# DeltaNet's triangular inverse in one decoder step: diagonal blocks of 32 instead of 16 solved on VectorE, and turned there

## Chip, core and metric

One NeuronCore of one Trainium2 chip runs the whole step as one program. The metric is the device time of one launch in microseconds (us). The engines carry the names of the profile: PE is TensorE (its weight loads are PEld), DVE is VectorE, ACT is ScalarE, POOL is GpSimd, and SP is the engine that issues every DMA of this kernel.

## What is computed

One layer of a decoder with three kinds of heads: 6 mLSTM heads (A), 6 gated DeltaNet heads (B) and 4 HGRN2 heads (C). The input is a prompt of 1024 tokens with 16 learned tokens in front of it, and 8 samples of 8 tokens. One projection of 2048 to 8984 columns gives all q, k, v and gate columns, and an output projection of 2048 x 2048 follows. Only the DeltaNet part is touched. Cut to what matters:

```python
def _gdn_segment(q, k, v, g, beta, S0, chunk):
    ...
    G = jnp.cumsum(gc, axis=-1)
    decay = jnp.exp(jnp.where(incl, G[..., :, None] - G[..., None, :], NEG_BIG))
    A = jnp.where(strict, bc[..., None] * decay * jnp.einsum('nbhtd,nbhsd->nbhts', kc, kc), 0.0)
    M = A + jnp.eye(c, dtype=A.dtype)
    rhs = jnp.concatenate([bc[..., None] * vc, (bc * jnp.exp(G))[..., None] * kc], axis=-1)
    sol = lax.linalg.triangular_solve(M, rhs, left_side=True, lower=True)
    U, Wk = sol[..., :HEAD_DIM], sol[..., HEAD_DIM:]
    ...
```

The kernel works in chunks of 128 tokens and builds the inverse of the unit triangular 128 x 128 matrix M of each chunk; the product of that inverse with the right-hand side follows.

## The kernel before

The tokens are worked through in two halves. The first half holds 592 columns: 512 prompt tokens in four chunks of 128, the 64 sample tokens and the 16 learned tokens (these 80 are a small fifth group). The second half holds the other 512 prompt tokens, four chunks. In each half the projection runs over the columns of the weights, head by head, in the order of `ORDER` (L39).

**The weight stream.** A piece is a 128 x 512 tile of weights. SP loads it into `wraw`, ACT rounds it to `whi`, DVE takes the rest into `wlo`, and PE multiplies the activations by both into `acc`. A piece is 24 matmuls in the first half (two accumulators) and 12 in the second. `wraw`, `whi` and `wlo` have four buffers each; `feed_ahead` (L273) splits three pieces ahead of PE and loads seven ahead.

**The heads' own work** runs beside this stream. Every head is a Python generator that issues a step and yields; `Weave` (L145) resumes it when a clock of estimated costs (`Clock`, L85, and `Engine.cost`, L112) says that its last step should be done. So PE's queue holds stream matmuls with a few matmuls of a head between them. PE works through its queue in order. The framework's scheduler then decides, before the run, in which order the instructions stand on the other engines.

**The inverse of a DeltaNet head** is in `gdn_scan` (from L1097). `Ball` holds the strictly triangular part B of M, for all chunks side by side (C of them: 5 in the first half, 4 in the second).

1. Each 16 x 16 diagonal block of B is written to DRAM (`db`, L1157, eight small DMAs), and its rows are read back so that each row stands in all partitions of its block (`Bb`, L1163, three DMAs).
2. `substitute()` solves all the diagonal blocks at once on DVE. `Yc` starts as an identity of 16 columns in each block, and 15 steps follow; each is a product `Yt` of a column of `Yc` with a row from `Bb`, and a subtraction from `Yc`. Each instruction needs the one before it. This is called the chain below.
3. One DVE instruction spreads `Yc` into the block-diagonal matrix Y (tag `s8`) with `submask`. After `substitute` the clock gets 8 us before the next step is issued.
4. `transpose_Y` turns the four chunks of Y on PE (`px`), ACT copies them to X (tag `s9`).
5. Doubling from 16 to 32: four full matmuls `pz` (B with X), DVE masks them with `zmask` into Z, four full matmuls `pyy`, DVE subtracts them from Y, and `transpose_Y` turns Y once more.
6. Doublings from 32 to 64 and from 64 to 128, with block matmuls `pz` and `pyy`; in the first of them `pyy` is computed for both X and Y.

Then a loop over the chunks carries the state (`pr`, `pw`, `pu`, `po`). In the first half, `first_chain` (the 80 tokens of the small group) is issued in pieces between the steps of the inverse. Before the inverse, `side()` issues `pqk` and the transposes `pvb` of v.

Of the kernel before, what the change touches and what calls it, by code (L numbers as in the profile page):

```python
# [6 lines left out]
F32 = mybir.dt.float32  # L7
F32R = mybir.dt.float32r
U8 = mybir.dt.uint8
BF16 = mybir.dt.bfloat16  # L10
AF = mybir.ActivationFunctionType
ALU = mybir.AluOpType
AX = mybir.AxisListType

P = 128
# [174 lines left out]
def hybrid_step(ctx, tc, i, o):  # L190
    nc = tc.nc
    ck = Clock()
    V, S, G, T = (Engine(ck, n, e) for n, e in (("V", nc.vector), ("S", nc.scalar), ("G", nc.gpsimd), ("T", nc.tensor)))
    DMA = nc.sync.dma_start
    weave = Weave(ck)

    cp = ctx.enter_context(tc.tile_pool(name="cp", bufs=1))
# [24 lines left out]
    ident = cp.tile([P, P], F32, name="ident")  # L222
# [284 lines left out]
    segment_mask(sm0, 1.0, 0.0, True)  # L507

    hmask = {}
    zmask = cp.tile([P, P], BF16, name="zmask")  # L510
    m = sq("io", "zm")
    G.memset(m, 0.0)
    v = m.rearrange("p (b x) -> p b x", x=2 * SUB)[:, :, 0:SUB]
    G.memset(v, 1.0)
    G.affine_select(v, v, pattern=[[-2 * SUB, P // (2 * SUB)], [0, SUB]], compare_op=ALU.is_ge, fill=0.0, base=-SUB, channel_multiplier=1)
    G.affine_select(v, v, pattern=[[2 * SUB, P // (2 * SUB)], [0, SUB]], compare_op=ALU.is_ge, fill=0.0, base=2 * SUB - 1, channel_multiplier=-1)
    G.tensor_copy(zmask, m)
# [28 lines left out]
    for r in range(0, P, 32):  # L546
        v = quadmask[r:r + 32]
# [4 lines left out]
    for r in range(0, P, NSAMP):  # L552
        v = rowmask[r:r + NSAMP]
# [39 lines left out]
    rows_dram = [dp.tile([5, HA, h], F32, name=f"rows{h}") for h in (WA, WB)]  # L593
# [173 lines left out]
        return cols_of[half.index][0:g.n, g.idx, kind, h:h + 1].to_broadcast([g.n, g.nt, width])  # L767

    def bc_row(tag, name, half, arr, h):
        t = row(tag, name)[:, 0:half.width]  # L770
        DMA(t, rows_dram[half.index][arr, h:h + 1, :].partition_broadcast(P))
        return t


# [322 lines left out]
    def gdn_scan(half, h, ck_, cq, cv, zs, Gb, eG, bb, st):  # L1097
        W = half.width
        gs, main = half.ggroups, half.gmain
        cols = cols_of[half.index]  # L1100
# [48 lines left out]
        for g, B in zip(gs, Bs):  # L1149
            n = g.n  # L1150
# [1 line left out]
            for c in range(g.nt):  # L1152
                T.matmul(g.psum(pk, n)[:, c], g.col(knT, c), g.col(knT, c), start=True, stop=True)
            V.tensor_tensor(B[0:n, :, 0:n], B[0:n, :, 0:n], g.psum(pk, n), op=ALU.mult)
        db = dp.tile([P // SUB, SUB, C, SUB], F32, name=f"db{half.index}{h}")
        for j in range(P // SUB):
            DMA(db[j], Ball[SUB * j:SUB * (j + 1), 0:C, SUB * j:SUB * (j + 1)])  # L1157
        dbf = db.rearrange("j s c t -> j (s c t)")
        Bb = []
        for lo, hi, tag in ((0, 6, "s7"), (6, 12, "s9"), (12, 15, "s6")):  # L1160
            w = C * SUB
            t = sp.tile([P, 512], F32, tag=tag, name="Bb", bufs=1)[:, 0:(hi - lo) * w]
            DMA(t, dbf[:, lo * w:hi * w].unsqueeze(1).to_broadcast([P // SUB, SUB, (hi - lo) * w]))  # L1163
            for x in range(hi - lo):
                Bb.append(t[:, x * w:(x + 1) * w].rearrange("p (c t) -> p c t", t=SUB))
        ready = ck.t["T"] + 7.0
        if half.first:
            kq = pair_tile()
# [4 lines left out]
        Ys, Xs = [], []  # L1173

        def transpose_Y(g, Y, X):
            n = g.n
            px = bank("px")
            for c in range(g.nt):
                T.transpose(g.psum(px, n)[:, c], Y[0:n, c, 0:n], ident[0:n, 0:n])
            S.copy(X[0:n, :, 0:n], g.psum(px, n))  # L1180

        def substitute():
            Yc = sp.tile([P, 5, SUB], F32, tag="Yc", name="Yc", bufs=1)[:, 0:C]
            tmp = sp.tile([P, 5, SUB], F32, tag="Yt", name="Yt", bufs=1)[:, 0:C]
            V.tensor_copy(Yc, subid.unsqueeze(1).to_broadcast([P, C, SUB]))
            for s_ in range(SUB - 1):
                r = slice(s_ + 1, SUB)
                V.tensor_tensor(tmp[:, :, r], Yc[:, :, s_:s_ + 1].to_broadcast([P, C, SUB - 1 - s_]), Bb[s_][:, :, r], op=ALU.mult)
                V.tensor_tensor(Yc[:, :, r], Yc[:, :, r], tmp[:, :, r], op=ALU.subtract)
                if s_ in (4, 9):  # L1190
                    ck.last = 0.0
                    yield
            for g in gs:
                nb = g.n // SUB
                Y = gt("8", g)
                V.tensor_tensor(Y[0:g.n, :, 0:g.n].rearrange("p c (j t) -> p c j t", t=SUB),
                                Yc[0:g.n, g.idx].unsqueeze(2).to_broadcast([g.n, g.nt, nb, SUB]),
                                submask[0:g.n, 0:g.n].rearrange("p (j t) -> p j t", t=SUB).unsqueeze(1).to_broadcast([g.n, g.nt, nb, SUB]),
                                op=ALU.mult)
                Ys.append(Y)  # L1200

# [59 lines left out]

        for _ in side():
            yield
        ck.last = max(ck.last, ready)
# [16 lines left out]
        py = main.psum(bank("pyy"))  # L1281
        for c in range(NC):
            T.matmul(py[:, c], Z[:, c], Y[:, c], start=True, stop=True)
        V.tensor_tensor(Y, Y, py, op=ALU.subtract)
        next(extra, None)
        yield
        transpose_Y(main, Y, X)
        next(extra, None)
        yield
        for hh in (32, 64):  # L1290
            pz = main.psum(bank("pz"))
            Z = gt("7", main)
            blocks = [(slice(b, b + hh), slice(b + hh, b + 2 * hh)) for b in range(0, P, 2 * hh)]
            for l, r in blocks:
                for c in range(NC):
                    T.matmul(pz[r, c, 0:hh], B[l, c, r], X[l, c, l], start=True, stop=True)
            for l, r in blocks:
                S.copy(Z[r, :, 0:hh], pz[r, :, 0:hh])
            yield
            py = main.psum(bank("pyy"))  # L1300
            for l, r in blocks:
                for c in range(NC):
                    T.matmul(py[l, c, 0:hh], Z[r, c, 0:hh], Y[r, c, r], start=True, stop=True)
                    if hh == 32:
                        T.matmul(py[r, c, hh:2 * hh], Y[r, c, r], Z[r, c, 0:hh], start=True, stop=True)
            for l, r in blocks:
                V.tensor_scalar(Y[l, :, r], py[l, :, 0:hh], -1.0, None, op0=ALU.mult)
                if hh == 32:
# [304 lines left out]
    for half, groups in zip(halves, group_lists):  # L1613
# [4 lines left out]
        for n, group in enumerate(groups):  # L1618
# [14 lines left out]
            cols = [col for _, _, col in group]  # L1633
# [48 lines left out]
    for half in halves:  # L1682
        toks = []
        for n, (c0, cnt) in enumerate(half.tiles):
            if half.first and n == 0:
                toks.append((0, NSAMP, xs_flat, ys_flat))
            else:
                a = HALF * half.index + c0
# [5 lines left out]
        for cg, some in OUT_UNITS[half.index]:  # L1694
# [79 lines left out]
```

## Time and profile before

| what | value |
|---|---|
| time, median of 3 runs (lowest to highest) | 2550.52 us (2545.99 to 2553.72) |
| the profiled execution's own time | 2546.89 us |
| its span in the trace | 2545.2 us |
| DVE busy | 1376.3 us (54%) |
| ACT busy | 1024.0 us (40%) |
| POOL busy | 552.8 us (22%) |
| DMA, mean over the span | 125 GB/s, 45.7% of 16 engines in the main queue |

Busy times are sums over instructions that ran on that engine; a wait is not busy time. Idle time of an engine that is not the bottleneck costs nothing. In the timeline, rows carry the start in us, the duration, the engine, the operation, its output and inputs, the shape and the count; the bracket at the end of a row is the idle time before it and what ended it.

### The profile page before, as it was taken

How to read it: one execution, taken by the hardware profiler on the slowest of the kernel's cores; microseconds unless marked ns; L12 is line 12 of the kernel's file. 1: busy time of each engine (PE TensorE's matmuls, PEld its weight loads, DVE VectorE, ACT ScalarE, POOL GpSimd, SP SyncE). 2: the span in 40 equal slices, each digit the busy share in tenths (PEclk: the TensorE clock that was granted, in tenths of full speed). 3: DMA queues.
4: the chain of work that ended last, by engine and by line, in shares of the span. 5: the costliest groups of instructions: out<-in, count | busy, mean ns of one | idle time of the engine just before them, and what ended most of it. 6: DMA issues, size and time to landing. Idle time of an engine off the chain costs nothing.

```text
span 2545.2 us, 43177 instructions
## 1 busy us (share of the span) xinstructions
PE 2482.4 (98%) x16022; PEld 2226.0 (87%) x16022; DVE 1376.3 (54%) x2881; ACT 1024.0 (40%) x2512; POOL 552.8 (22%) x722
## 2 busy tenths in 40 slices
PE   6899999999999999999999999999999999999998
PEld 5899999999999999999788888888888888888886
DVE  7665655665745655546754556454554545422435
ACT  5733434343434334334643434333443435322324
POOL 5331212320313312203320103110320102211201
PEclk9999999999999999999999999999999999999999
DMA  5634433555634343436443334433343438436735
GB/s 128 170 91 113 121 85 90 153 154 151 161 79 117 92 119 88 110 88 185 125 118 101 103 99 109 109 98 96 102 106 95 110 97 271 140 84 189 261 97 182
DMA packets 458319, 317.19 MB, mean 125 GB/s; under 512 B 56740, under 2 KB 402428, under 8 KB 457084
## 3 DMA queue, kind: packets, MB, share of 16 engines
q1 hardware_dynamic: 458108, 314.43, 45.7%
q8 instruction: 126, 2.06, 0.3%
q14 instruction: 85, 0.70, 0.1%
HBM read 268.93 MB, written 45.42 MB: 124 GB/s over the span
## 4 chain that ended last, share of the span: by engine, by line
PE 80%; issue 5%; DMA 4%; DVE 4%; POOL 3%; ACT 2%; SPq 0%; POOLq 0%; DVEq 0%; ACTq 0%
PE acc L136 59%; PE oacc L136 8%; PE pa L136 1%; DVE wlo L136 1%; PE po L136 1%; PE pyy L136 1%; PE pz L136 1%; POOL res L136 1%; PE pu L136 1%; PE nd L136 1%; POOL X L136 1%; DMA wraw<-in_w_in_dram 1%; PE poh L136 1%; DMA wraw<-in_w_out_dram 1%; DMA x<-in_x_prompt_dram 1%
## 5 line engine op out<-in xcount | busy, mean ns | idle before, releaser
L136 DVE TENSOR_TENSOR wlo<-wraw,whi 128x512 fp32r<-128x512 f32 x720 | 534.2, 746 | 639.4 <-ACT whi L136 628.3
L136 PE MATMUL acc<-hA,whi 128*128 128x288 f32 (+1 forms) x4544 | 822.9, 303 | 16.1 <-ACT whi L136 10.1
L136 ACT CAST whi<-wraw 128x512 fp32r<-128x512 f32 x720 | 442.2, 618 | 899.0 <-PE acc L136 584.1
L136 PE MATMUL acc<-hB,whi 128*128 128x512 f32 x2272 | 723.3, 400 | 1.5 <-ACT whi L136 1.5
L136 PEld LDWEIGHTS acc<-hA,whi 128*128 128x128 f32 x4544 | 675.4, 190 | 23.2 <-ACT whi L136 12.3
L136 PE MATMUL acc<-hA,wlo 128*128 128x288 f32 x2240 | 487.9, 298 | 0.2 <-DVE wlo L136 0.2
L136 PEld LDWEIGHTS acc<-hB,whi 128*128 128x128 f32 x2272 | 408.8, 188 | 79.7 <-ACT whi L136 3.4
L136 PE MATMUL acc<-hB,wlo 128*128 128x512 f32 x1120 | 439.7, 393 | 2.0 <-DVE wlo L136 2.0
L136 PEld LDWEIGHTS acc<-hA,wlo 128*128 128x128 f32 x2240 | 366.0, 189 | 1.5 <-DVE wlo L136 1.4
L136 PE MATMUL oacc<-whi,y 128*128 128x512 f32 x1088 | 343.8, 390 | 1.2 <-ACT whi L136 1.1
L136 PEld LDWEIGHTS acc<-hB,wlo 128*128 128x128 f32 x1120 | 210.2, 188 | 51.5 <-DVE wlo L136 5.6
L136 PEld LDWEIGHTS oacc<-whi,y 128*128 128x128 f32 x1088 | 204.3, 188 | 44.3 <-ACT whi L136 2.4
L136 PE MATMUL oacc<-wlo,y 128*128 128x512 f32 x576 | 224.6, 390 | 0.8 <-DVE wlo L136 0.7
L136 PEld LDWEIGHTS oacc<-wlo,y 128*128 128x128 f32 x576 | 108.2, 188 | 24.4 <-DVE wlo L136 2.3
L136 POOL TENSOR_TENSOR res<-res,fnw 128x512 f32<-128x512 f32 (+1 forms) x34 | 53.1, 1589 | 259.0 <-ACT oscr L136 259.0
L136 POOL TENSOR_TENSOR qd<-qT,emb 128x512 f32<-128x512 f32 x12 | 16.8, 1401 | 363.7 <-PE po L136 363.7
L136 POOL TENSOR_TENSOR y<-y,zs 128x592 fp32r<-128x592 f32 (+1 forms) x32 | 47.1, 1471 | 143.6 <-ACT zs L136 143.6
L136 DVE TENSOR_TENSOR Yt<-Yc,Bb 128x60 f32<-128x60 f32 (+8 forms) x180 | 36.9, 205 | 51.2 <-DMA Bb<-db 46.5
L136 POOL TENSOR_TENSOR hr<-hr,halfneg 128x4 f32<-128x4 f32 (+1 forms) x48 | 47.2, 984 | 56.0 <-DVE hr L136 55.0
L136 POOL TENSOR_TENSOR X<-Ex,hk 128x256 f32<-128x256 f32 (+1 forms) x40 | 38.5, 963 | 93.2 <-PE pa L136 75.5
L136 POOL TENSOR_TENSOR nrm<-nrm,halfneg 128x10 f32<-128x10 f32 x12 | 23.5, 1956 | 129.3 <-DVE nrm L136 129.3
L136 DVE TENSOR_TENSOR Sx<-Sx,lf 128x256 f32<-128x256 f32 (+2 forms) x60 | 34.0, 569 | 26.9 <-ACT Ex L136 24.9
(410 smaller groups left out, 2839.6 us busy)
## 6 DMA issues: line engine op xcount, KB each, us to landing
wraw<-in_w_in_dram SPq DMA_DIRECT2D x564, 256.0 KB
wraw<-in_w_out_dram SPq DMA_DIRECT2D x144, 256.0 KB
y<-y SPq DMA_DIRECT2D x16, 576.0 KB
px<-in_x_prompt_dram SPq DMA_DIRECT2D x32, 256.0 KB
out_dram<-sst SPq DMA_DIRECT2D x16, 512.0 KB
y<-zs SPq DMA_DIRECT2D x32, 256.0 KB
y<-y SPq DMA_DIRECT2D x32, 256.0 KB
res<-in_x_prompt_dram SPq DMA_DIRECT2D x32, 256.0 KB
```

The lines of the kernel that those rows point to most:

```text
L136: return f(out, *a, **k)
```

## The change

`SUB` goes from 16 to 32. The chain then solves blocks of 32, in 31 steps instead of 15, and rows are up to 32 columns wide. `db` becomes two DRAM tensors, one for the upper 16 rows of each block (32 columns wide) and one for the lower 16 rows (16 columns, since the other half of these rows is zero). All 31 rows read back don't fit in three tiles, so `spread_rows` puts them into tiles whose contents are no longer needed as well: those of the key columns (`Ck`), of the gate rows (`Gb`, `bb`), and in the first half that of the values (`Cv`), after `side()` has read them. The step from 16 to 32 on PE goes, with both `transpose_Y`, `zmask`, and the ACT copies. What the first remaining doubling needs transposed comes from one DVE instruction that turns every 32 x 32 block of `Yc` into `Xc`. POOL clears X and copies the blocks of `Xc` into it for the second doubling; the first reads `Xc` and `Yc` directly.

```diff
-SUB = 16
+SUB = 32
...
-        db = dp.tile([P // SUB, SUB, C, SUB], F32, name=f"db{half.index}{h}")
-        for j in range(P // SUB):
-            DMA(db[j], Ball[SUB * j:SUB * (j + 1), 0:C, SUB * j:SUB * (j + 1)])
-        dbf = db.rearrange("j s c t -> j (s c t)")
+        nb = P // SUB
+        db = [dp.tile([nb, SUB // 2, C, w], F32, name=f"db{half.index}{h}{w}") for w in (SUB, SUB // 2)]
+        for j in range(nb):
+            a = SUB * j
+            DMA(db[0][j], Ball[a:a + SUB // 2, 0:C, a:a + SUB])
+            DMA(db[1][j], Ball[a + SUB // 2:a + SUB, 0:C, a + SUB // 2:a + SUB])
         Bb = []
-        for lo, hi, tag in ((0, 6, "s7"), (6, 12, "s9"), (12, 15, "s6")):
...
+        def spread_rows(t, cols):
+
+            at_ = 0
+            while len(Bb) < SUB - 1:
+                x, s_ = divmod(len(Bb), SUB // 2)
+                w = C * (SUB >> x)
+                m = min((cols - at_) // w, SUB // 2 - s_ - x)
+                if m == 0:
+                    return
+                src = db[x].rearrange("j s c t -> j (s c t)")[:, s_ * w:(s_ + m) * w]
+                DMA(t[:, at_:at_ + m * w], src.unsqueeze(1).to_broadcast([nb, SUB, m * w]))
+                for _ in range(m):
+                    Bb.append(t[:, at_:at_ + w].rearrange("p (c t) -> p c t", c=C))
+                    at_ += w
+
+        for t in (ck_, Gb, bb):
+            spread_rows(t, UW)
+        for tag, cols_ in (("s7", 512), ("s9", 512), ("s6", 512), ("Bx", 320)):
...
             for s_ in range(SUB - 1):
                 r = slice(s_ + 1, SUB)
-                V.tensor_tensor(tmp[:, :, r], Yc[:, :, s_:s_ + 1].to_broadcast([P, C, SUB - 1 - s_]), Bb[s_][:, :, r], op=ALU.mult)
+                b = Bb[s_][:, :, r] if s_ < SUB // 2 else Bb[s_][:, :, s_ + 1 - SUB // 2:]
+                V.tensor_tensor(tmp[:, :, r], Yc[:, :, s_:s_ + 1].to_broadcast([P, C, SUB - 1 - s_]), b, op=ALU.mult)
                 V.tensor_tensor(Yc[:, :, r], Yc[:, :, r], tmp[:, :, r], op=ALU.subtract)
-                if s_ in (4, 9):
+                if s_ % 5 == 4:
                     ck.last = 0.0
                     yield
+            V.transpose(Xc.rearrange("p c t -> p (c t)"), Yc[:, main.at:main.at + NC].rearrange("p c t -> p (c t)"))
...
         ck.last += 8.0
         yield
-        Xs = [gt("9", main)]
-        transpose_Y(main, Ys[-1], Xs[-1])
         extra = first_chain() if half.first else iter(())
-        yield
-        B, Y, X = Bs[-1], Ys[-1], Xs[-1]
-        pz = main.psum(bank("pz"))
-        for c in range(NC):
-            T.matmul(pz[:, c], B[:, c], X[:, c], start=True, stop=True)
-        Z = gt("7", main)
-        V.tensor_tensor(Z, pz, zmask.unsqueeze(1).to_broadcast([P, NC, P]), op=ALU.mult)
...
-            T.matmul(py[:, c], Z[:, c], Y[:, c], start=True, stop=True)
-        V.tensor_tensor(Y, Y, py, op=ALU.subtract)
-        next(extra, None)
-        yield
-        transpose_Y(main, Y, X)
...
+        B, Y = Bs[-1], Ys[-1]
+        X = gt("9", main)[0:2 * SUB, :, 0:2 * SUB]
+        G.memset(X, 0.0)
+        for a in (0, SUB):
+            G.tensor_copy(X[a:a + SUB, :, a:a + SUB], Xc[a:a + SUB])
+        for hh in (SUB, 2 * SUB):
...
-                    T.matmul(pz[r, c, 0:hh], B[l, c, r], X[l, c, l], start=True, stop=True)
+                    T.matmul(pz[r, c, 0:hh], B[l, c, r], Xc[l, c] if hh == SUB else X[:, c], start=True, stop=True)
...
-                    if hh == 32:
-                        T.matmul(py[r, c, hh:2 * hh], Y[r, c, r], Z[r, c, 0:hh], start=True, stop=True)
+                    y = Yc[r, main.at + c] if hh == SUB else Y[r, c, r]
+                    T.matmul(py[l, c, 0:hh], Z[r, c, 0:hh], y, start=True, stop=True)
+                    if l.stop == SUB:
+                        T.matmul(py[r, c, hh:2 * hh], y, Z[r, c, 0:hh], start=True, stop=True)
```

Three places show how the instructions stand, all in the last DeltaNet head of the second half (called B5 below; the first is B0). PE first. Between the head's transposes `pvb` and the first matmul of its inverse the queue of before holds 75 stream matmuls; `s_22822` is Y, `s_22917` is X:

```order
L136 MATMUL acc<-hB_14798,wlo 128x512
L136 MATMUL px<-ident,s_22822 128x128 x4
L136 MATMUL acc<-hB_14798,whi 128x512
L136 MATMUL acc<-hB_14799,whi 128x512
L136 MATMUL acc<-hB_14798,wlo 128x512
L136 MATMUL acc<-hB_14587,whi 128x512
L136 MATMUL acc<-hB_14588,whi 128x512
L136 MATMUL acc<-hB_14587,wlo 128x512
L136 MATMUL pz<-s_22917,Ball 128x128 x4
```

In the changed kernel 102 stream matmuls stand between `pvb` and the first matmul of the inverse, which is now a block matmul on `Xc` (`s_23140` is Z):

```order
L135 MATMUL acc<-hB_14743,wlo 128x512
L135 MATMUL pz<-Xc,Ball 32x32 x8
L135 MATMUL acc<-hB_14812,whi 128x512
L135 MATMUL acc<-hB_14813,whi 128x512
L135 MATMUL acc<-hB_14812,wlo 128x512
L135 MATMUL acc<-hB_14812,whi 128x512
L135 MATMUL acc<-hB_14813,whi 128x512
L135 MATMUL acc<-hB_14812,wlo 128x512
L135 MATMUL pyy<-Yc,s_23140 32x32
```

The inverse enters PE's queue 27 stream matmuls later than before in the six heads of the second half. In the first half the counts are 132 before and 180 after in four heads, 138 and 192 in B0, 126 and 180 in B2.

On DVE, the end of the same head's chain before, where three `wlo` of the weight stream stand inside the chain in all:

```order
L136 TENSOR_TENSOR Yc<-Yc,Yt 128x4x4
L136 TENSOR_TENSOR wlo<-wraw,whi 128x512
L136 TENSOR_TENSOR Yt<-Yc,Bb 128x4x3
L136 TENSOR_TENSOR Yc<-Yc,Yt 128x4x3
L136 TENSOR_TENSOR Yt<-Yc,Bb 128x4x2
L136 TENSOR_TENSOR Yc<-Yc,Yt 128x4x2
L136 TENSOR_TENSOR Yt<-Yc,Bb 128x4
L136 TENSOR_TENSOR Yc<-Yc,Yt 128x4
L136 TENSOR_TENSOR s_22822<-Yc,submask 128x512
L136 TENSOR_TENSOR wlo<-wraw,whi 128x512 x3
L136 TENSOR_TENSOR s_22938<-pz,zmask 128x512
L136 TENSOR_TENSOR s_22822<-s_22822,pyy 128x512
```

And the end of the chain in the changed kernel, where seven `wlo` stand inside it (six in B1 of the first half):

```order
L135 TENSOR_TENSOR Yc<-Yc,Yt 128x4x4
L135 TENSOR_TENSOR Yt<-Yc,Bb 128x4x3
L135 TENSOR_TENSOR Yc<-Yc,Yt 128x4x3
L135 TENSOR_TENSOR Yt<-Yc,Bb 128x4x2
L135 TENSOR_TENSOR Yc<-Yc,Yt 128x4x2
L135 TENSOR_TENSOR Yt<-Yc,Bb 128x4
L135 TENSOR_TENSOR wlo<-wraw,whi 128x512
L135 TENSOR_TENSOR Yc<-Yc,Yt 128x4
L135 STREAM_TRANSPOSE Xc<-Yc 128x128
L135 TENSOR_TENSOR s_22998<-Yc,submask 128x512
L135 TENSOR_TENSOR wlo<-wraw,whi 128x512
L135 TENSOR_SCALAR s_22998<-pyy 32x4x32
```

The transposition follows the chain directly, ahead of the spreading of Y (`s_22998`); the two 128x512 instructions on `pz` and `pyy` are gone.

On SP, the DMAs of the same head's rows before:

```order
L1157 DMA db_22708<-Ball 64x1x16 x8
L237 DMA wraw<-in_w_in_dram 128x4x128
L1163 DMA Bb<-db_22708 128x1x384 x2
L1163 DMA Bb<-db_22708 128x1x192
L237 DMA wraw<-in_w_in_dram 128x4x128 x9
```

and in the changed kernel, after the eight small writes to `db`:

```order
L1151 DMA db_22847<-Ball 64x1x16
L236 DMA wraw<-in_w_in_dram 128x4x128
L1164 DMA Ck<-db_22846 128x1x512
L1164 DMA Gb<-db_22846 128x1x512
L1164 DMA bb<-db_22846 128x1x512
L1164 DMA Bb<-db_22846 128x1x512
L1164 DMA Bb<-db_22847 128x1x512
L1164 DMA Bb<-db_22847 128x1x448
L236 DMA wraw<-in_w_in_dram 128x4x128 x9
```

Six DMAs read 3008 values into each of the 128 partitions where three read 960 before; the first of them brings 512 values instead of 384. They stand at the same place of SP's queue, ahead of the same weight loads.

More of the change, by code (lines that the diff above doesn't have):

```diff
@@ L769, in bc_row @@
     def bc_row(tag, name, half, arr, h):
-        t = row(tag, name)[:, 0:half.width]
-        DMA(t, rows_dram[half.index][arr, h:h + 1, :].partition_broadcast(P))
+        t = row(tag, name)
+        DMA(t[:, 0:half.width], rows_dram[half.index][arr, h:h + 1, :].partition_broadcast(P))
         return t
@@ L1154, in gdn_scan @@
             V.tensor_tensor(B[0:n, :, 0:n], B[0:n, :, 0:n], g.psum(pk, n), op=ALU.mult)
-        db = dp.tile([P // SUB, SUB, C, SUB], F32, name=f"db{half.index}{h}")
-        for j in range(P // SUB):
-            DMA(db[j], Ball[SUB * j:SUB * (j + 1), 0:C, SUB * j:SUB * (j + 1)])
-        dbf = db.rearrange("j s c t -> j (s c t)")
-        Bb = []
-        for lo, hi, tag in ((0, 6, "s7"), (6, 12, "s9"), (12, 15, "s6")):
[L1161 to L1165, printed above, removed]
+        nb = P // SUB
[4 more added lines that the diff above has]
+            DMA(db[1][j], Ball[a + SUB // 2:a + SUB, 0:C, a + SUB // 2:a + SUB])
+        Bb = []
+        def spread_rows(t, cols):
[14 more added lines that the diff above has]
+        for tag, cols_ in (("s7", 512), ("s9", 512), ("s6", 512), ("Bx", 320)):
+            if len(Bb) < SUB - 1:
+                spread_rows(sp.tile([P, cols_], F32, tag=tag, name="Bb", bufs=1), cols_)
         ready = ck.t["T"] + 7.0
@@ L1172, in gdn_scan @@
         yield
[L1173 to L1180, printed above, removed]
+        Ys = []
+        Yc = sp.tile([P, 5, SUB], F32, tag="Yc", name="Yc", bufs=1)[:, 0:C]
+        Xc = sp.tile([P, NC, SUB], F32, tag="Xc", name="Xc", bufs=1)
         def substitute():
-            Yc = sp.tile([P, 5, SUB], F32, tag="Yc", name="Yc", bufs=1)[:, 0:C]
             tmp = sp.tile([P, 5, SUB], F32, tag="Yt", name="Yt", bufs=1)[:, 0:C]
@@ L1263, in gdn_scan @@
             yield
+        spread_rows(cv, UW)
         ck.last = max(ck.last, ready)
@@ L1268, in gdn_scan @@
         yield
-        Xs = [gt("9", main)]
-        transpose_Y(main, Ys[-1], Xs[-1])
         extra = first_chain() if half.first else iter(())
-        yield
-        B, Y, X = Bs[-1], Ys[-1], Xs[-1]
-        pz = main.psum(bank("pz"))
-        for c in range(NC):
-            T.matmul(pz[:, c], B[:, c], X[:, c], start=True, stop=True)
-        Z = gt("7", main)
-        V.tensor_tensor(Z, pz, zmask.unsqueeze(1).to_broadcast([P, NC, P]), op=ALU.mult)
-        next(extra, None)
-        yield
-        py = main.psum(bank("pyy"))
-        for c in range(NC):
-            T.matmul(py[:, c], Z[:, c], Y[:, c], start=True, stop=True)
-        V.tensor_tensor(Y, Y, py, op=ALU.subtract)
-        next(extra, None)
-        yield
-        transpose_Y(main, Y, X)
-        next(extra, None)
-        yield
-        for hh in (32, 64):
+        B, Y = Bs[-1], Ys[-1]
[4 more added lines that the diff above has]
+        for hh in (SUB, 2 * SUB):
             pz = main.psum(bank("pz"))
@@ L1295, in gdn_scan @@
                 for c in range(NC):
-                    T.matmul(pz[r, c, 0:hh], B[l, c, r], X[l, c, l], start=True, stop=True)
+                    T.matmul(pz[r, c, 0:hh], B[l, c, r], Xc[l, c] if hh == SUB else X[:, c], start=True, stop=True)
             for l, r in blocks:
                 S.copy(Z[r, :, 0:hh], pz[r, :, 0:hh])
+            next(extra, None)
             yield
@@ L1302, in gdn_scan @@
                 for c in range(NC):
-                    T.matmul(py[l, c, 0:hh], Z[r, c, 0:hh], Y[r, c, r], start=True, stop=True)
-                    if hh == 32:
-                        T.matmul(py[r, c, hh:2 * hh], Y[r, c, r], Z[r, c, 0:hh], start=True, stop=True)
+                    y = Yc[r, main.at + c] if hh == SUB else Y[r, c, r]
+                    T.matmul(py[l, c, 0:hh], Z[r, c, 0:hh], y, start=True, stop=True)
+                    if l.stop == SUB:
+                        T.matmul(py[r, c, hh:2 * hh], y, Z[r, c, 0:hh], start=True, stop=True)
             for l, r in blocks:
                 V.tensor_scalar(Y[l, :, r], py[l, :, 0:hh], -1.0, None, op0=ALU.mult)
-                if hh == 32:
+                if l.stop == SUB:
                     V.tensor_scalar(X[r, :, l], py[r, :, hh:2 * hh], -1.0, None, op0=ALU.mult)
```

15 lines of the change are left out of this document (3 added, 12 removed).

## The prediction

> **What bounds the kernel now.** I read the page first (busy time, then the chain that ended last), then the waits of PE, the groups of instructions by shape, and the timelines of single heads.
>
> ```profile
> span 2545.2 us, 43177 instructions
> PE 2482.4 (98%) x16022; PEld 2226.0 (87%) x16022; DVE 1376.3 (54%) x2881; ACT 1024.0 (40%) x2512; POOL 552.8 (22%) x722
> PE 80%; issue 5%; DMA 4%; DVE 4%; POOL 3%; ACT 2%; SPq 0%; POOLq 0%; DVEq 0%; ACTq 0%
> ...
> PE pt L136 <- DVE x L136: 12.0, 8, 6.6
> PE acc L136 <- ACT whi L136: 11.6, 12, 2.1
> PE px L136 <- DVE s L136: 2.6, 1, 2.6
> ```
>
> PE is busy for 98% of the span and carries 80% of the chain that ended last. The last rows are its waits (total, times, longest): some ten us each at most, and the inverse of DeltaNet costs one wait of 2.6 us in all twelve heads. So PE work that goes is time won, every wait added to PE is time lost in full, and DVE at 54% has room as long as it is not late. The question is whether it will be.
>
> **PE work removed.** Per head go eight transposes `px`, four full matmuls `pz`, four full `pyy`, and 8 of 32 records of the block matmuls `pyy`, since only the lower block pair needs both products now.
>
> ```profile
> L136 PE MATMUL px<-ident,s 128*128 128x128 f32 x96 | 14.4, 272 | 2.6 <-DVE s L136 2.6
> L136 PE MATMUL pz<-s,Ball 128*128 128x128 f32 x96 | 12.6, 275 | 0.0
> L136 PE MATMUL pyy<-s,s 128*128 128x128 f32 x96 | 12.6, 274 | 0.0
> L136 PE MATMUL pyy<-s,s 32*32 32x32 f32 x384 | 7.2, 194 | 0.0
> ```
>
> These are groups by shape over all twelve heads (busy us, mean ns of one). The first three add to 39.6 us and a quarter of the fourth is 1.8. Busy time includes the tail of a matmul over the next one, so I check against the pitch of weight loads in the timeline of the last head, B5:
>
> ```profile
> 2043.20 0.30 PEld L136 LDWEIGHTS acc<-hB,whi 128*128 128x128 f32 x2
> ...
> 2060.12 0.58 PEld L136 LDWEIGHTS px<-ident,s 128*128 128x128 f32 x4
> 2060.68 0.30 PEld L136 LDWEIGHTS acc<-hB,whi 128*128 128x128 f32 x2
> ...
> 2061.95 1.09 PEld L136 LDWEIGHTS pz<-s,Ball 128*128 128x128 f32 x8
> 2062.97 0.30 PEld L136 LDWEIGHTS acc<-hB,whi 128*128 128x128 f32 x2
> ```
>
> A set of `px` holds PE for 0.56 us and a set of `pz` for 1.02; `pyy` has as many records of the same length. That is 2 x 0.56 + 2 x 1.02 = 3.16 a head, 37.9 for twelve, and 39.7 with the 1.8. I take **39.5 us off**. The two masked DVE instructions and the ACT copies that go are off PE's path and count nothing.
>
> **The chain on DVE.** It gets 62 dependent instructions instead of 30. B5's chain before, first and last rows:
>
> ```profile
> 2048.90 0.22 DVE L136 TENSOR_TENSOR Yt<-Yc,Bb 128x60 f32<-128x60 f32 x1 [2.84 <-DMA Bb<-db]
> 2049.16 0.22 DVE L136 TENSOR_TENSOR Yc<-Yc,Yt 128x60 f32<-128x60 f32 x1
> 2049.30 0.68 DVE L136 TENSOR_TENSOR wlo<-wraw,whi 128x512 fp32r<-128x512 f32 x1
> 2049.90 0.21 DVE L136 TENSOR_TENSOR Yt<-Yc,Bb 128x56 f32<-128x56 f32 x1
> ...
> 2056.78 0.17 DVE L136 TENSOR_TENSOR Yt<-Yc,Bb 128x4 f32<-128x4 f32 x1
> 2056.98 0.17 DVE L136 TENSOR_TENSOR Yc<-Yc,Yt 128x4 f32<-128x4 f32 x1
> 2057.18 0.69 DVE L136 TENSOR_TENSOR s<-Yc,submask 128x512 f32<-128x512 f32 x1
> ```
>
> From start to start a link takes 0.26 us at 60 elements a partition and 0.20 at 4: 0.195 us + 1.02 ns an element. A `wlo` inside the chain makes a link 0.74 instead of 0.24, so it adds 0.5. Check: 30 x 0.195 + 960 elements x 1.02 ns + 3 x 0.5 = 8.33, and the rows give 2057.18 - 2048.90 = 8.28. The changed chain of the second half has 62 links and 2 x 4 x (1 + ... + 31) = 3968 elements: 12.1 + 4.05 = 16.1 us, plus seven `wlo`, 3.5: **19.6 us**. In the first half, with five groups, 4960 elements: 17.15, plus six `wlo`: 20.2. Links wider than 60 or 75 elements are not in the trace; the line is extended, and a tenth more or less per element moves the chain by 0.4 us.
>
> The transposition behind the chain is not in the trace either. It lies between a 4-element link (0.17) and a 128x512 instruction (0.69); at 128 elements the line gives 0.33, which I take. The Trainium skill (VectorE: DVE Perf Modes, The three transpose paths) puts a 128x128 bf16 transpose on VectorE at 311 ns, which would leave the sum where it is.
>
> The start of the chain is a DMA's landing. The first read-back grows from 192 to 256 KB a head in the second half; in a window over the landing of `Bb` the DMAs move 159 GB/s (last column; the share before it is that of the 16 DMA engines):
>
> ```profile
> 2045.77 1.89 SPq L1163 DMA_DIRECT2D Bb<-db  x3
> ```
> ```profile
> 2046.80:2050.30 3.50, 3.50 (x17) 2.92 (x16) 1.33 (x5) 0.76 (x2) 0.00 (x0) 1.00 0.53 159
> ```
>
> 64 KB more is 0.4 us (bounds 0 and 0.8, as if it had half the rate). In the first half the first read-back keeps its 240 KB. Later read-backs are 256 KB, 1.6 us each at that rate, against four steps of the chain that take 2.3 us or more; I cost them at nothing. All six are 1.54 MB, 9.7 us, and the next weight loads stand behind them; `wraw` is loaded seven pieces ahead, which covers that if the rate holds (see the rivals).
>
> **When PE comes for it.** The inverse now stands 27 stream matmuls later in PE's queue in the second half. 75 of them took 2060.12 - 2043.20 = 16.92 us, 0.226 each, so PE arrives 6.1 us later than before: in B5 at 2060.1 + 6.1 = 2066.2. The chain is ready at 2048.9 + 0.4 + 19.6 + 0.33 = 2069.2. **PE waits 3.0 us.** Heads B0, B2 and B4 have one more row load ahead of `Bb` in SP's queue, before and after; B4 shows it:
>
> ```profile
> 1923.92 0.59 PEld L136 LDWEIGHTS pvb<-ident,Cv 128*128 128x128 f32 x4
> ...
> 1941.39 0.58 PEld L136 LDWEIGHTS px<-ident,s 128*128 128x128 f32 x4
> ```
> ```profile
> 1931.61 0.22 DVE L136 TENSOR_TENSOR Yt<-Yc,Bb 128x60 f32<-128x60 f32 x1 [4.28 <-DMA Bb<-db]
> ...
> 1937.08 0.51 DVE L136 TENSOR_TENSOR Yc<-Yc,Yt 128x24 f32<-128x24 f32 x1
> ```
>
> Ready at 1931.6 + 0.4 + 19.6 + 0.3 + 0.3 (one link slowed from 0.2 to 0.5) = 1952.2, PE there at 1941.4 + 6.1 = 1947.5: 4.7 us. The second half: 3 x 3.0 + 3 x 4.7 = 23.1 us.
>
> In the first half B1 stands for the six heads, with 48 more stream matmuls:
>
> ```profile
> 351.25 0.56 PEld L136 LDWEIGHTS acc<-hA,whi 128*128 128x128 f32 x4
> ...
> 368.93 0.50 PEld L136 LDWEIGHTS px<-ident,s 128*128 128x128 f32 x4
> ```
> ```profile
> 356.85 0.24 DVE L136 TENSOR_TENSOR Yt<-Yc,Bb 128x75 f32<-128x75 f32 x1 [4.60 <-DMA Bb<-db]
> ```
>
> 132 matmuls in 17.68 us are 0.134 each; PE arrives at 368.9 + 6.4 = 375.4, the chain is ready at 356.9 + 20.2 + 0.3 = 377.4: 2.0 us, 12 for six heads. B2 waited 2.6 before (the row of PE's waits above) and its DVE queue holds other heads' work inside the chain; I add 2 for it. Waits in all: **37 us on**.
>
> After that, nothing is late: `wlo` of the next three pieces lie ahead of the transposition in DVE's queue, and POOL's two copies into X have over a stage of PE's time. So far 2546.9 - 39.5 + 37 = 2544.4.
>
> **The clock of PE.** The change puts gaps of 2 to 5 us into PE twelve times. Two gaps of before show what may follow:
>
> ```profile
> 98.60:102.10 3.50, 1.39 (x10) 1.15 (x9) 0.51 (x1) 2.82 (x7) 0.95 (x1) 0.99 0.96 310
> 102.10:105.50 3.40, 3.40 (x16) 3.31 (x15) 3.28 (x9) 3.14 (x7) 0.00 (x0) 0.51 0.45 117
> ...
> 584.90:587.50 2.60, 0.03 (x1) 0.06 (x2) 2.50 (x8) 0.00 (x0) 0.41 (x1) 1.00 0.21 68
> 587.50:591.00 3.50, 3.50 (x29) 3.50 (x30) 2.17 (x5) 0.59 (x1) 0.00 (x0) 1.00 0.56 140
> ```
>
> After 2.1 us without PE work in 3.5, the granted clock is 0.51 for the next 3.4 us and 16 matmuls run; after 2.6 us (the wait of B2) it stays at 1.00 and 29 run in as long. A drop costs 13/29 of 3.4 us, 1.5 us. I count all three gaps like B4's and half of the other nine: 7.5 x 1.5 = 11 us. The Trainium skill (TensorE: Matmul & The Clock Gate, What's actually happening) says that the clock falls after an idle window of some 3.4 us in a free-running grid. By that, only gaps near 5 us could hold a whole window, less than every second time, and the sum would be near 2547; the first pair of rows speaks against so mild a rule.
>
> **Sum.** 2546.9 - 39.5 + 37 + 11 = 2555.4, 8.5 above the profiled execution's own time. That lies 3.6 below the median of the runs, 2550.5; moved to it, the forecast is 2559, rounded to **2560**.
>
> **The rivals.**
> (1) *Slower by little, no clock drop:* waits as above, clock at 1.00 throughout: 2544.4, on the median 2548, no change. The rows of B2 speak for it.
> (2) *The chain is in time, faster:* its whole wait depends on some 3 us a head. If wide links cost less than the line, or PE comes later than counted, the waits vanish and PE's saving stays: 2507 without any, 2526 with half of them; on the median 2511 to 2530. It decides at a chain of 16.5 us in the second half where I count 19.6. The line's fit to 0.05 us speaks against it; that every second term is an extension speaks for it.
> (3) *Weight loads behind the read-backs:* 1.54 to 1.93 MB go ahead of them per head. If the rate falls to 110 GB/s, the queue takes 14 us or more, the fourth `wlo` inside the chain waits for its `wraw`, and with it the chain. Two us more a head: 2560 + 24 = 2584. For it speaks the share of 0.53 that 159 GB/s already takes; against it that no `wlo` waits for a DMA before.
> (4) *The removed matmuls hide behind something:* PE's saving would shrink; their rows show no idle time of PE before them, so I give it little.
>
> **Chances.** Forecast 0.45, (1) 0.20, (2) 0.23, (3) 0.10, (4) 0.02. A measurement tells about 0.3% (7.7 us) from no change: faster is below 2543, slower above 2558. The forecast, with half a us of error a head either way, lies between 2549 and 2574 and is slower in three of four. Faster: 0.24. Slower: 0.34 + 0.10 + some of (4), 0.46. Within: 0.30. The range holds the forecast, (1), the upper part of (2) and (3): 2522 to 2588.
>
> **What would show it.** The groups `px` and the full `pz` and `pyy` gone, and the chain's span near 19.6 us in B5: the first two steps. A new row among PE's waits, `pz` on DVE `Xc`, twelve times, 37 us in all, with 3 and 4.7 us alternating in the second half: the third. Clock below 1.00 right behind these waits: the fourth. No such row, and a time near 2510, would prove (2); a DVE row `wlo` or `Yt` waiting on ACT or a DMA inside the chain would prove (3). The forecast is wrong if the scheduler's order on DVE leaves more than these seven `wlo` in the chain's way, or if the wide links leave the line.

## The result and the profile after

The changed kernel takes **2699.45 us** in the median (2697.36 to 2705.18, four runs) beside 2549.11 us of the kernel before: a ratio of **1.0592, 95% interval 1.0568 to 1.0616**. The profiled execution took 2698.44 us, its span is 151.5 us longer than before. The forecast was 2560 us, with a range of 2522 to 2588: the sign was right, and the size wrong by 140 us.

The page of the changed kernel, then PE's waits, then one row of the waits of all engines (total us, times, longest):

```profile
span 2696.7 us, 42879 instructions
...
PE 2511.1 (93%) x15638; PEld 2234.2 (83%) x15638; DVE 1453.9 (54%) x3241; ACT 1013.3 (38%) x2488; POOL 571.9 (21%) x753
```
```profile
PE pz L135 <- DVE Xc L135: 73.2, 12, 7.3
PE acc L135 <- ACT whi L135: 41.4, 19, 5.3
PE acc L135 <- DVE wlo L135: 28.0, 7, 8.9
```
```profile
ACT whi L135 <- DMA wraw<-in_w_in_dram: 209.7, 47, 15.8
```

DVE is no busier in share than before, and PE's share falls from 98% to 93%. PE's first wait is the forecast one, for `Xc`, twelve times, but twice as long. The next two are new: the weight stream itself stops, 69.4 us beside 13.8 before (11.6 and 2.2). The last row names what it waits for: ACT waits 209.7 us for `wraw` to land, and up to 15.8 us at once. Before, this row was

```profile
ACT whi L136 <- DMA wraw<-in_w_in_dram: 28.1, 12, 7.0
```

The six heads of the second half look alike: in each, PE waits 4.4 to 5.3 us at `acc` and, ten to twelve us later, 4.9 to 7.0 us for `Xc`. B5 on SP, then on DVE, then on PE (start, duration, and in the bracket the idle time before and its end):

```profile
2182.94 0.57 SPq L1164 DMA_DIRECT2D Ck<-db  x1
2183.56 0.54 SPq L1164 DMA_DIRECT2D Gb<-db  x1
2184.15 0.50 SPq L1164 DMA_DIRECT2D bb<-db  x1
2184.69 7.23 SPq L1164 DMA_DIRECT2D Bb<-db  x3
```
```profile
2190.20 0.29 DVE L135 TENSOR_TENSOR Yt<-Yc,Ck 128x124 f32<-128x124 f32 x1 [6.83 <-DMA Ck<-db]
2190.53 0.29 DVE L135 TENSOR_TENSOR Yc<-Yc,Yt 128x124 f32<-128x124 f32 x1
...
2199.91 0.23 DVE L135 TENSOR_TENSOR Yc<-Yc,Yt 128x72 f32<-128x72 f32 x1
2205.66 0.69 DVE L135 TENSOR_TENSOR wlo<-wraw,whi 128x512 fp32r<-128x512 f32 x1 [5.51 <-ACT whi L135]
...
2215.58 0.31 DVE L135 STREAM_TRANSPOSE Xc<-Yc 128x128 f32<-128x128 f32 x1
```
```profile
2205.68 1.22 PE L135 MATMUL acc<-hB,whi 128*128 128x512 f32 x2 [4.44 <-ACT whi L135]
...
2216.04 0.84 PE L135 MATMUL pz<-Xc,Ball 32*32 32x32 f32 x16 [5.91 <-DVE Xc L135]
```

The six read-backs stand in SP's queue ahead of the weights. PE runs out of weights and waits 4.4 us; the fourth `wlo` stands inside the chain, waits for the same weights, and makes the chain 5.5 us later; so PE waits a second time, for `Xc`. In the first half the rows of other heads stand behind the read-backs too. In B0's chain DVE stands still for one of them:

```profile
241.95 0.24 DVE L135 TENSOR_TENSOR nm<-nm,am 80x80 f32<-80x80 f32 x1 [12.01 <-DMA nm<-rows]
```

How fast the read-backs run is in two windows (the last three columns are PE's clock, the busy share of the 16 DMA engines, and GB/s). The first lies in the changed kernel, where nothing else moves; the second in the kernel before, over its own read-backs:

```profile
2188.30:2194.30 6.00, 6.00 (x29) 4.95 (x28) 3.59 (x13) 0.92 (x2) 0.00 (x0) 1.00 0.26 101
```
```profile
2047.10:2049.10 2.00, 2.00 (x11) 1.65 (x10) 0.20 (x1) 0.62 (x1) 0.00 (x0) 1.00 0.48 165
```

0.48 of 16 engines are 7.7 and 0.26 are 4.2. Before, a read-back took its rows from eight blocks of DRAM, one for each block of 16 partitions; now it takes them from four. The 1.54 MB of a head need 15.2 us at 101 GB/s.

The Trainium skill (DMA: Bandwidth & Descriptors, Why a DMA increments its semaphore by 16 and not by 1) says that a DMA is shared among the largest number of engines up to 16 that divides the outermost counts of both sides. By that, eight blocks give 8 engines and four give 4; both rows agree.

The clock follows the two waits. The windows behind B5's second wait:

```profile
2215.90:2219.40 3.50, 3.36 (x22) 2.56 (x22) 1.26 (x2) 0.51 (x2) 1.25 (x2) 0.50 0.62 143
2219.40:2222.80 3.40, 3.40 (x31) 2.58 (x31) 0.85 (x3) 0.00 (x0) 0.00 (x0) 0.50 0.02 7
2222.80:2226.00 3.20, 3.20 (x14) 2.24 (x13) 0.69 (x1) 0.80 (x2) 0.00 (x0) 0.52 0.00 0
```

Half the clock lasts here for three stretches of 3.2 to 3.5 us behind the wait, where the forecast counted one. Over the whole run the mean granted clock is 0.961 beside 0.996.

### The profile page after: what moved, and what is told of

The parts are those of the page before. It is cut to its first block, busy times and chain, and to the rows that moved or that the text cites. A ratio compares the mean times of both kernels' runs of the same rounds, so it can differ in the third digit from the quotient of the medians.

```text
span 2696.7 us, 42879 instructions
## 1 busy us (share of the span) xinstructions
PE 2511.1 (93%) x15638; PEld 2234.2 (83%) x15638; DVE 1453.9 (54%) x3241; ACT 1013.3 (38%) x2488; POOL 571.9 (21%) x753
## 5 line engine op out<-in xcount | busy, mean ns | idle before, releaser
L135 PE MATMUL acc<-hA,whi 128*128 128x288 f32 (+1 forms) x4544 | 832.2, 306 | 17.1 <-ACT whi L135 12.6
L135 PE MATMUL acc<-hB,whi 128*128 128x512 f32 x2272 | 748.3, 409 | 29.3 <-ACT whi L135 28.9
L135 PEld LDWEIGHTS acc<-hA,whi 128*128 128x128 f32 x4544 | 686.1, 193 | 24.4 <-ACT whi L135 15.4
L135 PEld LDWEIGHTS acc<-hB,whi 128*128 128x128 f32 x2272 | 425.4, 194 | 116.1 <-ACT whi L135 32.6
L135 PE MATMUL acc<-hA,wlo 128*128 128x288 f32 x2240 | 495.0, 301 | 27.4 <-DVE wlo L135 27.4
L135 PE MATMUL acc<-hB,wlo 128*128 128x512 f32 x1120 | 449.5, 401 | 0.8 <-DVE wlo L135 0.5
L135 PEld LDWEIGHTS acc<-hB,wlo 128*128 128x128 f32 x1120 | 216.4, 193 | 51.9 <-DVE wlo L135 5.9
L135 DVE TENSOR_TENSOR Yc<-Yc,Yt 128x100 f32<-128x100 f32 (+55 forms) x372 | 88.5, 238 | 11.0
L135 PE MATMUL pz<-Xc,Ball 32*32 32x32 f32 x192 | 9.8, 233 | 73.2 <-DVE Xc L135 73.2
L135 PEld LDWEIGHTS pz<-Xc,Ball 32*32 32x32 f32 x192 | 8.6, 144 | 77.3 <-issue 77.3
```

What stands on the lines that cost most here:

```text
L135: return f(out, *a, **k)
```

## The experiments

Theory A: the read-backs run at a low rate because they come from four blocks, and hold up the weights queued behind them. Theory B, the rival: the chain of 62 links is too late by itself. Each ratio is to the kernel before, with its 95% interval.

**e1, the rows of the first read-back used again.**

```diff
-        for t in (ck_, Gb, bb):
-            spread_rows(t, UW)
...
+        spread_rows(ck_, UW)
+        n0 = len(Bb)
+        while len(Bb) < SUB - 1:
+            Bb.append(Bb[len(Bb) % n0] if len(Bb) < SUB // 2 else Bb[len(Bb) % n0][:, :, SUB // 2:])
```

> The changed kernel with only the first of the six read-backs of each head (four rows in the second half, three in the first); the other 27 or 28 steps of the chain use these rows again, so the rest of the rows is left out of the computation. The chain keeps its 62 links. Theory A (the read-backs are slow and hold up the weight loads queued behind them): PE's wait for whi and wlo at acc falls from 69 us to below 20, the 5.5 us gap before a wlo inside B5's chain is gone, PE's wait for Xc falls from 73 us to 10 to 35, and the time is 2545 to 2580. Theory B (the chain of 62 links is too long by itself): the wait for Xc stays above 60 us and the time above 2640.

Measured: 2610.86 us, 1.0243 (1.0221 to 1.0265). PE's waits, SP, and B5's chain:

```profile
PE pz L135 <- DVE Xc L135: 53.0, 12, 6.3
PE acc L135 <- ACT whi L135: 13.9, 12, 2.2
...
PE acc L135 <- DVE wlo L135: 3.9, 8, 1.0
```
```profile
2096.63 0.57 SPq L1164 DMA_DIRECT2D Ck<-db  x1
```
```profile
2102.75 0.29 DVE L135 TENSOR_TENSOR Yt<-Yc,Ck 128x124 f32<-128x124 f32 x1 [5.37 <-DMA Ck<-db]
...
2122.28 0.31 DVE L135 STREAM_TRANSPOSE Xc<-Yc 128x128 f32<-128x128 f32 x1
```

The weight waits are gone with the five later read-backs, and 89 us with them. But the wait for `Xc` stayed above A's 35 us, and the time above A's range: neither theory has it all. The chain itself takes 2122.28 - 2102.75 = 19.5 us. Its start is late: 6.1 us after the issue of the first read-back, where the kernel before shows 2048.90 - 2045.77 = 3.1. B5 is the extreme case: in the median of the twelve heads it is 6.1 against 4.2. The first read-back also comes from four blocks. An estimate from these rows: twelve starts that are 1.9 us later, where the forecast had 0.4 in six heads, would bring its 37 us to about 57, beside the 53.0 measured.

**e2 and e3, the kernel before with more reading.** Its chain stays; four reads a head are added, of 2048 or 2368 values into each partition, from k = 4 or 8 blocks.

```diff
...
+        dbx = db.rearrange("(a j) s c t -> a (j s c t)", a=k)
+        m = 592 if half.first else 512
+        Bx = sp.tile([P, m], F32, tag="Bx", name="Bx", bufs=1)
+        for t in (ck_, Gb, bb, Bx):
+            DMA(t[:, 0:m], dbx[:, 0:m].unsqueeze(1).to_broadcast([k, P // k, m]))
```

> The kernel before, whose chain is unchanged, with four more read-backs a head behind its own three: 2048 values (2368 in the first half) into each partition, read from four blocks of DRAM, 32 partitions from each, as the changed kernel reads. Theory A: PE waits for whi and wlo at acc grow from 14 us to 50 to 80, the clock drops behind them, and the time is 2600 to 2660. Theory B: nothing is late, 2545 to 2560.

> As the run before it, the same bytes, but read from eight blocks of DRAM, 16 partitions from each, as the kernel before reads. Theory A with the number of blocks as the cause of the low rate: the reads run at about 180 GB/s instead of 100 and hold the weights for about 6 us a head instead of 10, so that most of the waits are gone: 2550 to 2590. Theory A with the bytes alone as the cause: as the run before it, within 10 us. Theory B: 2545 to 2560.

Measured: **2624.93 us with four blocks, 1.0306 (1.0290 to 1.0321); 2550.64 us with eight, 1.0012 (1.0003 to 1.0021)**. The same bytes cost 77 us or 2. In e2 PE's waits are not at `acc`, where they were expected, but at the inverse, and ACT's waits for weights have grown:

```profile
PE pz L136 <- ACT s L136: 26.9, 10, 4.5
PE px L136 <- DVE s L136: 25.8, 11, 8.5
```
```profile
ACT whi L136 <- DMA wraw<-in_w_in_dram: 167.3, 36, 12.8
```

ACT stands before a `whi` whose weights have not landed, and the copy of `px` that `pz` needs is queued behind it. In e3 that row is

```profile
ACT whi L136 <- DMA wraw<-in_w_in_dram: 78.2, 28, 6.8
```

and the reads run at

```profile
2053.00:2057.90 4.90, 4.90 (x24) 4.04 (x22) 3.26 (x15) 1.43 (x3) 0.00 (x0) 1.00 0.50 150
```

half of the 16 engines: eight blocks. The two kernels differ in one thing more. In all twelve heads the scheduler put one of the added reads (`Ck`) ahead of `Bb` in SP's queue in e2, and behind it in e3. So e2's chain also starts later (in B5 6.7 us after the issue of `Bb`, in e3 3.1), and its waits at `px` belong to that in part. In both, the weight loads stand behind all seven reads, so that ACT's waits for them, 167.3 and 78.2 us, do not hang on this place. The pair shows that reads from fewer blocks hold up the weights of the kernel before as well; how much of the 77 us is the order, it does not show. In e5 and e6 below the reads stand in the same order.

**e4, the inverse later in PE's queue.** `ck.last += 8.0` becomes `ck.last += 20.0`.

> The changed kernel with 20 us instead of 8 us given to the clock behind the chain, so that the inverse stands later in PE's queue. Theory A: the wait for Xc falls from 73 us to below 15, the waits for whi and wlo at acc stay near 69 us, and the time is 2590 to 2640. Theory B: the wait for Xc is all that matters, and with its clock drops gone the time is 2540 to 2580.

Measured: 2645.03 us, 1.0383 (1.0366 to 1.0401), 5 us above A's range and far above B's.

```profile
PE acc L135 <- ACT whi L135: 41.7, 19, 5.5
PE acc L135 <- DVE wlo L135: 28.8, 9, 9.5
```

The wait for `Xc` is out of the list, and the waits for weights are what they were: the two are separate costs. The time falls by 54 us, less than the 73 of the wait, and steps of the later loop (`pw`, `pu`, `puh`) now meet PE late, 23.9 us in all where the changed kernel shows 1.2.

**e5 to e7, the blocks written to DRAM once, twice, four times.** DVE gathers the diagonal blocks into two tiles that are free until the chain starts, and K DMAs write each; the read-backs then come from 4, 8 or 16 blocks. The rest is the changed kernel.

```diff
...
-        for j in range(nb):
-            a = SUB * j
-            DMA(db[0][j], Ball[a:a + SUB // 2, 0:C, a:a + SUB])
-            DMA(db[1][j], Ball[a + SUB // 2:a + SUB, 0:C, a + SUB // 2:a + SUB])
+        for x, t in enumerate((Yt, Yc)):
+            w = SUB >> x
+            t = t.rearrange("p c t -> p (c t)")[:, 0:C * w]
+            for j in range(nb):
+                a = SUB * j
+                V.tensor_copy(t[a:a + SUB].rearrange("p (c t) -> p c t", t=w), Ball[a:a + SUB, 0:C, a + SUB - w:a + SUB])
+            for k in range(K):
+                DMA(db[x][:, k].rearrange("j s c t -> j s (c t)"), t)
...
-                DMA(t[:, at_:at_ + m * w], src.unsqueeze(1).to_broadcast([nb, SUB, m * w]))
+                DMA(t[:, at_:at_ + m * w], src.unsqueeze(1).to_broadcast([nb * K, SUB // K, m * w]))
```

> The changed kernel with the writes to db gathered: DVE first copies the diagonal blocks side by side into Yt and Yc, two DMAs write them, and the read-backs are as in the changed kernel, from four blocks. Theory A (the rate of reads from four blocks is the cause): the rate stays at 100 GB/s, so the waits for whi and wlo at acc stay above 50 us and the time is 2650 to 2700, the shorter writing being worth at most 3 us a head. Theory D (the eight small writes to db ahead of the weight loads are the cause): acc waits fall below 30 us, 2600 to 2640.

> The same, but each block is written to DRAM twice (four DMAs), so that the six read-backs come from eight blocks, 16 partitions from each. Theory A: the reads run at 180 to 200 GB/s, the gap before a wlo inside the chain goes, acc waits fall below 30 us, the wait for Xc to 20 to 45 us, with the clock drops that belong to it: 2560 to 2600. Theory D: as the run with one copy.

> The same with four copies (eight DMAs write), so that the read-backs come from 16 blocks. Theory A: the reads run at 250 GB/s or more, acc waits are near those of the kernel before (14 us), the wait for Xc is 10 to 40 us since the chain itself (19.6 us) is still 2 to 3 us too long a head: 2545 to 2590.

| copies, blocks | time, us | ratio, 95% interval | PE waits for `Xc`, us | PE waits at `acc` (`whi` of ACT, `wlo`), us |
|---|---|---|---|---|
| changed kernel, 4 blocks | 2699.45 | 1.0592 (1.0568 to 1.0616) | 73.2 | 69.4 |
| 1, 4 blocks | 2641.78 | 1.0376 (1.0345 to 1.0407) | 47.0 | 52.3 |
| 2, 8 blocks | 2568.40 | 1.0076 (1.0057 to 1.0095) | 27.0 | 22.1 |
| 4, 16 blocks | 2559.70 | 1.0049 (1.0029 to 1.0068) | 29.2 | 14.4 |

The second copy alone takes 73 us off, though it adds two writes, and e6 and e7 lie in theory A's ranges. Theory D falls as the cause of the waits for weights: with one copy they stay above 50 us. But the gathering was worth more than expected (58 us instead of at most 36), and e5's time lies 8 us below theory A's range and 2 above D's. In e5's B5 the first read-back is issued 3.0 us after `Ball` is finished, in the changed kernel, with its eight writes, 6.2 us; why that earlier start is worth so much is not shown. The kernel before has the eight writes too, and no run gathers them there. In e7, with eight writes again, the first read-back is issued after 5.9 us, nearly as late as with the ungathered writes. With 16 blocks the read-backs run at

```profile
2060.40:2064.30 3.90, 3.90 (x19) 3.24 (x18) 2.21 (x8) 1.24 (x3) 0.00 (x0) 1.00 0.91 276
```

and B5's first link starts 3.3 us after the issue of its rows, as before; the chain has no hole:

```profile
2058.85 0.57 SPq L1172 DMA_DIRECT2D Ck<-db  x1
```
```profile
2062.18 0.29 DVE L135 TENSOR_TENSOR Yt<-Yc,Ck 128x124 f32<-128x124 f32 x1 [1.19 <-DMA Ck<-db]
...
2081.16 0.31 DVE L135 STREAM_TRANSPOSE Xc<-Yc 128x128 f32<-128x128 f32 x1
```

**e8, four copies and a later entry** (14 us instead of 8 behind the chain).

> The same with four copies, and 14 us instead of 8 us given to the clock behind the chain. Theory A: neither weights nor Xc are late, no clock drops are added, and the 39.5 us of PE work show: 2508 to 2530, faster than the kernel before. Theory B (the chain costs more than PE saves wherever it stands): no faster than 2545.

Measured: 2540.08 us, 0.9966 (0.9951 to 0.9980): faster than before, but 10 us short of A's range. No wait for `Xc` is left; in the first half other steps of the neighbouring heads now meet PE late:

```profile
PE py L135 <- DVE s L135: 7.1, 4, 2.2
PE pum L135 <- ACT meta L135: 5.6, 3, 2.2
```

**e9, the kernel before without its doubling from 16 to 32.**

```diff
-        pz = main.psum(bank("pz"))
...
-        V.tensor_tensor(Y, Y, py, op=ALU.subtract)
...
-        transpose_Y(main, Y, X)
```

> The kernel before without its step from 16 to 32: the four full matmuls pz, the four full pyy, the two masked DVE instructions and the second transposition px with its copy are left out of the computation; the chain of 30 links and the read-backs stay. It measures the PE work that the change removes (all but one set of px and a quarter of the block pyy). By the sum of the prediction a head saves 2 x 1.02 + 0.56 = 2.6 us, 31 us in all: a time of 2514 to 2522. By the time for which PE is occupied by these matmuls beyond its neighbours, in the second half of the runs with four copies, it is about 2.06 us a head, 25 us: 2522 to 2529. If something else hides it (rival 4): above 2535.

Measured: 2520.95 us, 0.9888 (0.9873 to 0.9903): 28.5 us of the 2547.58 of before, 24.7 to 32.4 by the interval. Both sums lie within it, and the median between them; rival 4 falls.

**e10 to e12, the entry tuned.** e8 with 8 us (e10) or 11 us (e11) in the first half and 14 us in the second; e12 is e11 with two copies.

> Four copies, with 14 us given to the clock behind the chain in the second half alone, and 8 us in the first, since the run with 14 us in both took 6 us longer in its first half (1195.9 against 1189.7 us) and 23.6 less in its second (940.0 against 963.6). If the two halves add up: 1189.7 + 940.0 + 392 and the rest, 2532 to 2538. If the first half's gain is not repeatable: 2538 to 2548.

> The same with 11 us in the first half. The waits for Xc of the first half (4.7 us at the longest, in B2) go mostly, and if its collisions with other heads' steps do not come in turn: 2522 to 2534. If they come with any later entry, as with 14 us: 2536 to 2545.

> As the run with 11 and 14 us behind the chain, but with two copies in DRAM instead of four: four DMAs write instead of eight, and the read-backs come from eight blocks. With the entry late enough, reads at the rate of the kernel before (about 180 GB/s) should hide: 2522 to 2534, level with four copies. If the slower reads still hold weights or other heads' rows back: 2535 to 2550.

| run | time, us | ratio, 95% interval |
|---|---|---|
| e10: 8 and 14 us, four copies | 2537.27 | 0.9951 (0.9939 to 0.9964) |
| e11: 11 and 14 us, four copies | **2524.64** | **0.9910 (0.9896 to 0.9923)** |
| e12: 11 and 14 us, two copies | 2534.14 | 0.9947 (0.9933 to 0.9961) |

e10 lies where the two halves add up. e11 is faster than both kernels, by 23 us and by 175 us. It gathers its writes and the kernel before does not; in that kernel PE's waits at `acc` and at `px` come to 16.4 us, and how much of them gathering would save is not tested. Of the waits for `Xc` e11 keeps one:

```profile
PE pz L135 <- DVE Xc L135: 2.4, 1, 2.4
```

e12 lies 9.5 us above it, at the very edge of what was expected for reads that hide: once the entry is late enough, the step from eight to 16 blocks still counts. One wait of PE has grown from e11, the first row, to e12, the second:

```profile
PE acc L135 <- DVE wlo L135: 1.2, 4, 0.4
```
```profile
PE acc L135 <- DVE wlo L135: 8.2, 14, 1.7
```

These 7.0 us are not the whole account. The profiled spans differ by 10.4 us: PE's idle time grew by 5.8 us in all, since other waits shrank, and its busy time by 4.6 us for the same 15638 matmuls. Where these come from is open.

## Why the prediction was wrong, step by step

The failed step is the price of the read-backs: "Later read-backs are 256 KB, 1.6 us each at that rate", "I cost them at nothing", and `wraw` loaded seven pieces ahead, "which covers that if the rate holds". The 159 GB/s were read over reads from eight blocks and carried over to reads from four. They ran at 101 GB/s. The row quoted for it held the warning: a share of 0.53 is 8.5 of 16 engines, and the change halves the number of blocks. It was taken for a load on the engines, not for the number of engines that such a read uses.

| term, us | forecast | changed kernel | four copies (e7) |
|---|---|---|---|
| PE work removed | -39.5 | -36 | -36 |
| wait for `Xc` | +37 | +73.2 | +29.2 |
| waits for weights at `acc` | 0 | +55.6 | +0.6 |
| lower clock (in the runs: the rest) | +11 | +59 | +19 |
| sum, on the span of before | +8.5 | +151.5 | +13.2 |

The -36 is e9's 28.5 for a part that the forecast puts at 31, scaled to its 39.5; its interval makes it -31 to -41. The clock's term is what is left, and no run measures it by itself. An estimate from the mean clocks (0.996 before, 0.961 in the changed kernel, 0.988 in e7) fits it: if the clock is either 1.00 or 0.50, the two kernels spend about 190 and 41 us more at 0.50 than the kernel before. A PE that worked all through would lose half of that, 95 and 20; some of this time falls into the waits, where nothing is lost.

- **Work removed, the chain, the transposition:** as forecast. The chain takes 19.5 us in e1 for 19.6, the transposition 0.31 us for 0.33, and a link of 124 elements 0.33 us (2190.20 to 2190.53) where the extended line gives 0.32. In e7 one `wlo` less stands in the chain, and it takes 19.0.
- **The start of the chain:** forecast 0.4 us later in the second half (at most 0.8) and not at all in the first. From the issue of the first read-back to the first link, the median of the twelve heads is 4.2 us before and 6.1 in e1; with one, two and four copies it is 6.2, 4.4 and 3.7. It follows the number of blocks.
- **The wait for `Xc`:** the mechanism, the place and the twelve times were right. Its size holds roughly where the reads are fast (29.2 us in e7, with one `wlo` less in B5's chain) and doubles where they are slow: the chain starts later and, in B5, gets a hole of 5.5 us. The forecast alternation shows in e7 as well: 3.1, 2.5, 4.2, 2.0, 3.7 and 1.5 us in the second half.
- **"After that, nothing is late":** wrong, but ahead of it: the stream's own weights are late, once a head.
- **The clock:** 1.5 us for each of 7.5 drops was too little. In B5, where the second wait ends 10.4 us after the first, half the clock lasts for some ten us behind it.
- **Rival 3** named this mechanism, and even the fourth `wlo` and 110 GB/s; the sign that it gave, a `wlo` that waits on ACT inside the chain, is the row with 5.51 above. It got a chance of 0.10 and 2 us a head. The 5.5 us in the chain, the wait at `acc` beside it and the clock come to 89 us between the changed kernel and e1, 7.4 a head. What spoke against it, "that no `wlo` waits for a DMA before", says nothing of a read that runs on half the engines.
- Theory B keeps a part: with fast reads PE still waits 29 us for the chain, and the kernel is at 1.0049. A later place in PE's queue removes all but 2.4 us of that (e11). That e7 comes within 5 us of the forecast's sum is luck in part: the wait is 8 us smaller than forecast and the clock's term 8 us larger.

That reading from more blocks takes most of the added waits for weights away is shown by e5 against e6, and by e2 against e3 with the order of one read changed as well. That a later entry helps is shown; why 11 us in the first half is better than 8 and 14 was only read from the waits of e8.

## What to carry to other kernels

A rate read from a trace belongs to a shape: before it is used for another transfer, look at how many DMA engines the share column stands for, and whether the change alters that number. When rows are broadcast from DRAM, writing the source in several copies, so that 16 blocks are read, can cost less than reading from few. A transfer that stands ahead of a prefetch stream in one queue was paid here by what the stream feeds, and twice, since the stream's split stood inside the chain as well.

## What the runs showed of the hardware

Read-backs ran at 101 GB/s from four blocks, 150 to 165 from eight (not the 180 that the expectations had) and 276 from 16, at shares of 0.26, 0.48 to 0.50 and 0.91 of the engines. With the blocks, the runs change the number of partitions that read one block (32, 16, 8); that the engines are the limit rests on the share, not on a run that changes one of the two alone. SP is held up as well: its issues of `Bb` took 0.61 us in the median before, and in the changed kernel

```profile
L1164 SPq DMA_DIRECT2D Bb<-db x48: 548/2264/5782, 216.9 to 2189.5; - x48
```

(min, median and max in ns). So the weight loads behind them were issued late as well: in B5 the next one 9.0 us after the first read-back (2182.94 to 2191.97), in e7 3.9. The median is 2.31 us in e5, from four blocks too, 0.57 in e6 and 0.60 in e7.
